# Hybrid pool, GLA and attention block: softmax division moved from the probabilities to the outputs, once a pair and half, through a DRAM round trip on GpSimd's queue

## The chip, the cores and the metric

The kernel runs on one core of a Trainium2 chip. Its time is the device time of one launch, in microseconds (us), and lower is better. Engines are named as in the profile: PE is TensorE's matrix unit and PEld its weight loads, DVE is VectorE, ACT is ScalarE, POOL is GpSimd, and SP is the queue that issues most of the transfers. "L615" is line 615 of the kernel before.

## What is computed

One transformer-like layer on 1024 tokens of width 1024, all in fp32: RMSNorm, one input projection, three token mixers side by side (pooling, gated linear attention, forgetting attention), an output projection, a residual, then RMSNorm, a SwiGLU feed-forward of width 2816, a residual and a last RMSNorm. The change touches the forgetting attention alone: eight heads of 64, causal, with a softmax.

```
def fox_mixer(q, k, v, f_logit, b_f):            # 8 heads of 64, 1024 tokens
    logf = log_sigmoid(f_logit + b_f); F = cumsum(logf over time)
    s = (q * 64**-0.5) @ k.T + F[query] - F[key]
    s = where(key <= query, s, -inf)
    p = softmax(s)                               # exp(s - max) / sum
    return p @ v
...
mix = concatenate([y_pool, y_gla, y_fox]); x = x + mix @ w_o
```

## The kernel before

fp32 products are made of three matmuls on a high and a low part of each operand (hi·hi, hi·lo, lo·hi), so nearly every operand is split once by ACT (copy to fp32r) and once by DVE or POOL (the rest). The program is written in one order, and a scheduler with a timeline of its own then sets the order on each engine; rings and pools of buffers limit it. What follows goes by that final order.

The attention works on pairs of heads, p = 0 to 3; a is the head of the pair (its rows are 64a to 64a+63). For one pair `fox_attend` makes eight items (a, m), one for every 256 queries. An item does this, in `fox_item`:

- scores: for its two blocks of 128 queries, PE multiplies Q with K and with KL, K's low part (tile `s`, L575, L576), and adds the causal mask (L578); DVE adds the key's F, stores into `pb` and takes the minimum (L580); ACT makes exp, and sums each row (L584).
- division: DVE's reciprocal of the two sums (L587), then `pb` times it, the first block on POOL (L590), the second on DVE (L592).
- turning: PE transposes `pb` in pieces of 128x128 (tile `pt`, L601), ACT and DVE split them into `pp` (L603, L604).
- output: PE multiplies with V's high and low parts side by side into the one bank of tag `o` (L615); ACT copies its lower half out (L618, `ot`), and DVE adds the upper half (L621, `y`). With that the bank is free for the next item.

PSUM holds 3 banks for `s`, 2 for `pt`, 1 for `o` and 2 for `gm` (projections). In SBUF the rings are "p" (six `pb`), "pp" (three), "fb" (two, the rows of F), "wr" (two raw weights on their way in) and "w" (their split parts).

Around the attention of pair p stand projections that PE can do in between: `zq`, `zk` of the next pair (48 matmuls of 512 columns each), `psv` (the values of heads 4 to 7, 192 matmuls of 256 columns, with the weights `wfv_0`, `wfv_1`, made between pairs 1 and 2 in the program), and `pxa`, `pxb`, the output projection (192 matmuls of 512 columns each). Their raw weights come through the ring "wr"; POOL makes the low part of zq, zk and wfv (L119). A finished pair's output `y` is split by ACT (L273) and DVE (L274) and stored in DRAM (`keep_mix`); the last pair's output is split at once into `last_mix` (L624, L625). After the output projection each block of 128 tokens is normed (`norm2`: L720, L722 with the gain row `ln2b` that POOL's queue loads at L714) and turned by PE (`n2pt`, L727). Then come the feed-forward's matmuls (`m`, L774, and `d`, L1030).

Of the kernel before, what the change touches and what calls it, by code (L numbers as in the profile page):

```python
# [18 lines left out]
P = 128  # L19
# [12 lines left out]
def tile_hybrid_block(ctx: ExitStack, tc, x, w_fv, w_gv, w_zt, w_o, w_gu, w_down, ln, w_pool, w_a3, chans, b_f, consts, out):  # L32
    nc = tc.nc
    ACT, DVE, POOL, PE, SP = nc.scalar, nc.vector, nc.gpsimd, nc.tensor, nc.sync
# [4 lines left out]
    dpool = ctx.enter_context(tc.tile_pool(name="dp", bufs=1, space=bass.MemoryType.DRAM))  # L39
# [10 lines left out]
    def G(name, dtype=F32):  # L50
        i = idle.pop(0)
        t_ = big.tile([P, 1024], dtype, tag=f"g{i}", name=name)
        where[name] = i
        return t_

    def free(*names):
        for n in names:
            idle.append(where.pop(n))

    def R(name, dtype=F32, tag="p"):  # L60

# [50 lines left out]
    def PS(tag, name):  # L112
        return pst.tile([P, 512], F32, tag=tag, name=name, bufs=BANKS[tag])
# [22 lines left out]
    def half(name, dtype=F32):  # L136
        return rng.tile([P, 512], dtype, tag="tmp", name=name, bufs=2)
# [25 lines left out]
    def names_T(name):  # L163
        return [f"{name}{k}_{c}_{h}" for k in range(4) for c in range(2) for h in range(2)]
# [105 lines left out]
    def keep_mix(k, y):  # L270

        hi = G(f"mh{k}", F32R)
        ACT.activation(hi, y, AF.Copy)  # L273
        DVE.tensor_tensor(out=y, in0=y, in1=f(hi), op=ALU.subtract)  # L274
# [17 lines left out]
    last_mix = []  # L292
# [253 lines left out]
                    POOL.tensor_copy(t_[a][own[1 - a], csl], f(t_[a][own[a], csl]))  # L546
        return Q, K, KL

    def fox_item(p, a, m, ops, fb, V, Y):

        Q, K, KL = (t_[a] for t_ in ops)
        nm = f"{p}_{a}_{m}"
        rows = slice(64 * a, 64 * a + 64)
        Pb, Ws = [], []
        l, rl = S(f"l{nm}", 2), S(f"rl{nm}", 2)
        for i in range(2):
            qb = 2 * m + i
            W = P * (qb + 1)
            nh = 1 if W <= 512 else 2
            w = W // nh  # L560
            qs = slice(qb * P, (qb + 1) * P)
            mn = S(f"mn{nm}_{i}")
            if m >= 2:
                pb = R(f"pb{nm}_{i}")
            elif i == 0:
                pb2 = R(f"pb{nm}")
                pb = pb2[:, 0:512]
            else:
                pb = pb2[:, 512:1024]
            top = 3.0e38  # L570
            for h in range(nh):
                s = PS("s", f"s{nm}_{i}_{h}")
                ks = slice(h * w, (h + 1) * w)
                last = h == nh - 1
                PE.matmul(s[:, 0:w], Q[:, qs], K[:, ks], start=True, stop=False)  # L575
                PE.matmul(s[:, 0:w], Q[:, qs], KL[:, ks], start=False, stop=not last)  # L576
                if last:
                    PE.matmul(s[:, w - P:w], identr, maskr, start=False, stop=True)  # L578
                t_ = mn if last else S(f"mw{nm}_{i}")
                DVE.tensor_tensor_reduce(out=pb[:, ks], in0=s[:, 0:w], in1=fb[:, ks], scale=1.0, scalar=top,  # L580
                                         op0=ALU.add, op1=ALU.min, accum_out=t_)
                top = t_[:, 0:1]

            ACT.activation(pb[:, 0:W], pb[:, 0:W], AF.Exp, bias=mn[:, 0:1], scale=-1.0, accum_out=l[:, i:i + 1])  # L584
            Pb.append(pb)
            Ws.append(W)
        DVE.reciprocal(rl, l)  # L587
        for i, (pb, W) in enumerate(zip(Pb, Ws)):
            if i == 0:
                POOL.tensor_tensor(out=pb[:, 0:W], in0=pb[:, 0:W], in1=rl[:, 0:1].broadcast_to([P, W]), op=ALU.mult)  # L590
            else:
                DVE.tensor_scalar(out=pb[:, 0:W], in0=pb[:, 0:W], scalar1=rl[:, 1:2], scalar2=None, op0=ALU.mult)  # L592
        o = PS("o", f"o{nm}")
        for n in range(m + 1):
            pt = PS("pt", f"pt{nm}_{n}")
            pp = R(f"pp{nm}_{n}", F32R, tag="pp")
            cut = P if n == m else 0
            for b in range(2):
                for i in range(b if cut else 0, 2):
                    o0 = 256 * b + P * i - cut * b  # L600
                    PE.transpose(pt[:, o0:o0 + P], Pb[i][:, (2 * n + b) * P:(2 * n + b + 1) * P], ident)  # L601
            w = 512 - cut
            ACT.activation(pp[:, 0:w], pt[:, 0:w], AF.Copy)  # L603
            DVE.tensor_tensor(out=pp[:, 512:512 + w], in0=pt[:, 0:w], in1=f(pp[:, 0:w]), op=ALU.subtract)  # L604
            for b in range(2):
                kb = 2 * n + b
                o0 = cut * b
                v_ = V[p % 2][kb // 4][:, kb % 4, a]
                ph = pp[:, 256 * b:512 - o0] if b else pp[:, 0:256]
                pl = pp[:, 768:1024 - o0] if b else pp[:, 512:768]  # L610
                both = (o[:, o0:256], v_.rearrange("p s e -> p (s e)"), ph)
                high = (o[0:64, o0:256], v_[:, 0], pl)
                last = kb == 2 * m + 1
                for n_, args in enumerate((high, both) if last else (both, high)):
                    PE.matmul(*args, start=(kb == 0 and n_ == 0), stop=(last and n_ == 1))  # L615
        tmp = half(f"ot{nm}")
        ot, oy = tmp[0:64, 0:256], tmp[:, 256:512]
        ACT.activation(ot, o[64:128, 0:256], AF.Copy)  # L618
        if p < 3:
            oy = Y[:, m * 256:(m + 1) * 256]  # L620
        DVE.tensor_tensor(out=oy[rows], in0=o[0:64, 0:256], in1=ot, op=ALU.add)  # L621
        if p == 3:
            hi, lo = (last_mix[m // 2][rows, h, (m % 2) * 256:(m % 2 + 1) * 256] for h in range(2))
            ACT.activation(hi, oy[rows], AF.Copy)  # L624
            POOL.tensor_tensor(out=lo, in0=oy[rows], in1=f(hi), op=ALU.subtract)  # L625

    def fox_attend(p, ops, V, Y):
        fbs = []
        for a in range(2):
            fb = R(f"fb{p}_{a}", tag="fb")  # L630
            SP.dma_start(fb, Fd[2 * p + a:2 * p + a + 1, :].broadcast_to([P, T]))
            fbs.append(fb)
        for a, m in ([(a, m) for a in range(2) for m in range(4)] if p < 3 else [(a, m) for m in (1, 0, 3, 2) for a in range(2)]):
# [40 lines left out]
    V = fox_values(0, (B.within(1), o_[0][:1], o_[0][1:], o_[1][:1], o_[1][1:] + B.turned(0), B.turned(1), (), ()))  # L674
    for k in range(8):
        keep_wo(k)
    ops = fox_qk(0)
    free("gv0", "gv1", "attb0", "attb1")
    for p in range(4):
        if p == 3:  # L680
            last_mix += [G(f"mix7_{g}", F32R).rearrange("p (h t) -> p h t", h=2) for g in range(2)]
        Y = G(f"y{p}") if p < 3 else None
        fox_attend(p, ops, V, Y)
        done = [f"{n}{p}_{a}" for n in ("q", "k", "kl") for a in range(2)] + [f"v{p}_{i}" for i in range(2)]
        if p == 1:
# [12 lines left out]
    ws = [fetch_wo(k) for k in range(4)]
# [284 lines left out]
    sums = {}  # L983
# [139 lines left out]
```

## Time and profile before

| what | before |
|---|---|
| median of 3 runs | 1176.26 us (1174.48 to 1177.74) |
| the profiled execution | 1175.42 us |
| its span, first to last instruction | 1173.7 us |
| granted TensorE clock, mean | 0.992 |
| busy: PE, DVE, ACT, POOL | 1136.0, 828.2, 536.0, 340.4 us |
| first projections and gated mixer | 0 to 202 us |
| attention with its projections and the output projection | 202 to 541 us |
| feed-forward | 541 to 1173 us |

Busy times are sums over the span, and the stages have different limits, so a share of busy time says little by itself: an instruction that leaves an engine is worth time only where PE was waiting for that engine. A row of a view reads: line, engine, operation, output<-input, shape, count | busy us, mean ns | idle time of that engine just ahead, and what ended it.

### The profile page before, as it was taken

Reading aid. Unit: us, or ns where it says so; the run is one execution under the profiler, and the core shown is the slowest. Engines: PE = TensorE matmul, PEld = TensorE weight load, DVE = VectorE, ACT = ScalarE, POOL = GpSimd, SP = SyncE. Lnnn points to the kernel's source line nnn. Section 1 sums busy time; section 2 is a strip of 40 time slices with the busy share of each in tenths; the row PEclk is TensorE's granted clock in tenths of the full one; section 3 lists DMA queues with packets and bytes.
Section 4 is the critical chain, followed back from the end, with each engine's and each line's share of the span. In section 5 each row is a group of like instructions: output and inputs, shape, how many; then the busy total and the mean of one; then the engine's idle time right before and its main releaser. Section 6 shows DMA issues by size and latency. Waiting matters only on the chain.

```text
span 1173.7 us, 15953 instructions
## 1 busy us (share of the span) xinstructions
PE 1136.0 (97%) x5928; PEld 958.5 (82%) x5928; DVE 828.2 (71%) x1365; ACT 536.0 (46%) x970; POOL 340.4 (29%) x260
## 2 busy tenths in 40 slices
PE   6999998999999999998999999999999999999996
PEld 5877878889978888886888888888888888888875
DVE  6697364387746866579997767767686685876686
ACT  6454233466654644456453433444344344334345
POOL 2231123343322413210302221022201370660784
PEclk9999999999999999999999999999999999999999
DMA  7121184411203734431323332242314688333233
GB/s 250 37 73 52 59 295 174 176 39 35 91 18 126 305 132 159 173 112 46 117 86 129 101 115 88 101 134 82 135 54 152 224 322 293 103 95 102 86 112 143
DMA packets 57692, 150.45 MB, mean 128 GB/s; under 512 B 5080, under 2 KB 5512, under 8 KB 57616
## 3 DMA queue, kind: packets, MB, share of 16 engines
q1 hardware_dynamic: 57184, 147.87, 36.5%
q0 software_dynamic: 432, 1.57, 0.4%
q8 instruction: 46, 0.75, 0.3%
q14 instruction: 30, 0.25, 0.1%
HBM read 105.09 MB, written 44.34 MB: 127 GB/s over the span
## 4 chain that ended last, share of the span: by engine, by line
PE 76%; DVE 4%; DMA 1%; issue 1%; POOL 1%; ACT 1%; SPq 0%; POOLq 0%; DVEq 0%; ACTq 0%
PE m L774 36%; PE d L1030 15%; PE pxa L144 4%; PE pxb L144 3%; PE o L615 3%; PE pt L601 2%; PE psv L152 2%; PE s L575 1%; PE s L576 1%; PE zq3p L152 1%; PE zq0p L152 1%; PE zq2p L152 1%; PE zk1p L152 1%; PE zk2p L152 1%; PE zk0p L152 1%
## 5 line engine op out<-in xcount | busy, mean ns | idle before, releaser
L774 PE MATMUL m<-hA_0h,wr 128*128 128x512 f32 x616 | 214.7, 391 | 1.2 <-ACT hr L729 1.2
L774 PE MATMUL m<-hA_1h,wr 128*128 128x512 f32 x616 | 214.9, 389 | 0.0
L774 PEld LDWEIGHTS m<-hA_0h,wr 128*128 128x128 f32 x616 | 116.1, 189 | 25.8 <-ACT hr L729 1.6
L774 PEld LDWEIGHTS m<-hA_1h,wr 128*128 128x128 f32 x616 | 115.8, 188 | 24.2
L1030 PE MATMUL d<-lw,ha 128*128 128x512 f32 x308 | 119.9, 389 | 0.9 <-DVE lw L880 0.9
L774 PE MATMUL m<-hA_0l,wr 128*128 128x512 f32 x308 | 120.3, 391 | 0.0
L774 PE MATMUL m<-hA_1l,wr 128*128 128x512 f32 x308 | 119.9, 389 | 0.0
L1030 PE MATMUL d<-hw,ha 128*128 128x512 f32 x308 | 119.3, 389 | 0.0
L1030 PE MATMUL d<-hw,la 128*128 128x512 f32 x308 | 118.4, 389 | 0.0
L756 ACT ACTIVATE wr<-ws 128x512 fp32r<-128x512 f32 x110 | 69.5, 632 | 101.5 <-DVE ws L755 50.1
L826 POOL TENSOR_TENSOR cg<-cu,cu 128x512 f32<-128x512 f32 x11 | 19.7, 1795 | 302.8 <-DVE cu L803 266.7
L757 DVE TENSOR_TENSOR wr<-ws,wr 128x512 fp32r<-128x512 f32 x110 | 76.8, 704 | 20.6 <-ACT wr L756 20.5
L880 DVE TENSOR_TENSOR la<-ra,ha 128x1024 fp32r<-128x1024 f32 (+1 forms) x42 | 57.2, 1368 | 32.0 <-ACT ha L879 24.7
L590 POOL TENSOR_TENSOR pb<-pb,rl 128x128 f32<-128x128 f32 (+3 forms) x32 | 39.0, 1222 | 117.5 <-DVE rl L587 108.9
L872 POOL TENSOR_TENSOR rw<-wd,wd 128x512 f32<-128x512 f32 x33 | 59.0, 1815 | 47.7 <-PE d L1030 47.6
L879 ACT ACTIVATE ha<-ra 128x1024 fp32r<-128x1024 f32 (+1 forms) x42 | 41.3, 987 | 65.6 <-DMA ra<-cd 56.8
L1030 PEld LDWEIGHTS d<-lw,ha 128*128 128x128 f32 x308 | 57.8, 188 | 13.3 <-DVE lw L880 1.3
L604 DVE TENSOR_TENSOR pp<-pt,pp 128x512 fp32r<-128x512 f32 (+1 forms) x80 | 50.2, 631 | 25.7 <-ACT pp L603 25.3
L774 PEld LDWEIGHTS m<-hA_0l,wr 128*128 128x128 f32 x308 | 58.1, 189 | 12.0
L774 PEld LDWEIGHTS m<-hA_1l,wr 128*128 128x128 f32 x308 | 58.0, 188 | 12.0
L1030 PEld LDWEIGHTS d<-hw,la 128*128 128x128 f32 x308 | 57.8, 188 | 12.1
L1030 PEld LDWEIGHTS d<-hw,ha 128*128 128x128 f32 x308 | 57.8, 188 | 11.9
(398 smaller groups left out, 2690.6 us busy)
## 6 DMA issues: line engine op xcount, KB each, us to landing
ra<-cd SPq DMA_DIRECT2D x35, 512.0 KB, 3.9
wu<-in_w_gu_dram SPq DMA_DIRECT2D x22, 512.0 KB, 4.6
wg<-in_w_gu_dram SPq DMA_DIRECT2D x22, 512.0 KB, 3.7
wd<-in_w_down_dram SPq DMA_DIRECT2D x22, 512.0 KB, 6.4
mix<-mixs SPq DMA_DIRECT2D x14, 512.0 KB, 5.3
cd<-cg SPq DMA_DIRECT2D x11, 512.0 KB, 6.3
cd<-cs SPq DMA_DIRECT2D x11, 512.0 KB, 3.4
cd<-cu SPq DMA_DIRECT2D x11, 512.0 KB, 3.3
```

Source lines behind the costliest of these rows:

```text
L144: PE.matmul(ps, a, b, start=(n == 0), stop=(n == last))
L152: PE.matmul(ps, a, b, start=(i == 0 and n == 0), stop=(i == len(terms) - 1 and n == 2))
L590: POOL.tensor_tensor(out=pb[:, 0:W], in0=pb[:, 0:W], in1=rl[:, 0:1].broadcast_to([P, W]), op=ALU.mult)
L604: DVE.tensor_tensor(out=pp[:, 512:512 + w], in0=pt[:, 0:w], in1=f(pp[:, 0:w]), op=ALU.subtract)
L615: PE.matmul(*args, start=(kb == 0 and n_ == 0), stop=(last and n_ == 1))
L756: ACT.activation(hi, src, AF.Copy)
L757: DVE.tensor_tensor(out=lo, in0=src, in1=f(hi), op=ALU.subtract)
L774: PE.matmul(ps, a, b, start=(n == 0), stop=(n == 11))
L872: POOL.tensor_tensor(out=raw_[:, j * 512:j * 512 + 512], in0=wd[h0, j0 + j][:, e0, :], in1=wd[h1, j0 + j][:, e1, :], op=op)
L879: ACT.activation(hi[:, sl], src, AF.Copy)
L880: DVE.tensor_tensor(out=lo[:, sl], in0=src, in1=f(hi[:, sl]), op=ALU.subtract)
L1030: PE.matmul(banks[t], a[:, o], b[:, ns], start=(j0 + j == 0 and m == 0), stop=(j0 + j == NF // 2 - 1 and m == 2))
```

## The change

`pb` is no longer divided. The sums of a pair are kept in one tile of 16 columns, and the outputs are divided at the end of the pair, in two halves g of 512 tokens: `divide` takes the reciprocal of the eight columns (DVE), turns them with PE (128x8 to 8x128, through a `pt` bank), copies them out with ACT, writes the 4 KB to DRAM on POOL's queue, reads them back twice with a step of zero over 64 partitions (tile `rb`, in a buffer of the ring "wr"), and multiplies `y` by them on POOL. The last pair makes its first half after its first four items; its split into `last_mix` comes after the division and is made once a half. The copy of the lower half of the `o` bank goes from ACT to DVE. In the program, `divide` of pair p stands behind the projections of pair p+1 and ahead of `keep_mix`.

```
-    def fox_item(p, a, m, ops, fb, V, Y):
+    def fox_item(p, a, m, ops, fb, V, Y, sums):
...
-            ACT.activation(pb[:, 0:W], pb[:, 0:W], AF.Exp, bias=mn[:, 0:1], scale=-1.0, accum_out=l[:, i:i + 1])
+            ACT.activation(pb[:, 0:W], pb[:, 0:W], AF.Exp, bias=mn[:, 0:1], scale=-1.0, accum_out=sums[:, col(a, qb)])
...
-        DVE.reciprocal(rl, l)
-        for i, (pb, W) in enumerate(zip(Pb, Ws)):
-            if i == 0:
-                POOL.tensor_tensor(out=pb[:, 0:W], in0=pb[:, 0:W], in1=rl[:, 0:1].broadcast_to([P, W]), op=ALU.mult)
-            else:
-                DVE.tensor_scalar(out=pb[:, 0:W], in0=pb[:, 0:W], scalar1=rl[:, 1:2], scalar2=None, op0=ALU.mult)
...
-        ACT.activation(ot, o[64:128, 0:256], AF.Copy)
-        if p < 3:
-            oy = Y[:, m * 256:(m + 1) * 256]
-        DVE.tensor_tensor(out=oy[rows], in0=o[0:64, 0:256], in1=ot, op=ALU.add)
+        ot = half(f"ot{nm}")[0:64, 0:256]
+        DVE.tensor_copy(ot, o[64:128, 0:256])
+        DVE.tensor_tensor(out=Y[rows, m * 256:(m + 1) * 256], in0=o[0:64, 0:256], in1=ot, op=ALU.add)
+    Ld = dpool.tile([4, 2, 2, 512], F32, name="Ld")
+    def divide(p, Y, sums, g):
+        rw = R(f"rb{nm}", tag="wr")
+        rl, rt, rb, gs = S(f"rl{nm}", 8), rw[0:8, 512:640], rw[:, 0:512], slice(g * 512, g * 512 + 512)
+        DVE.reciprocal(rl, sums[:, 8 * g:8 * g + 8])
+        pt = PS("pt", f"ptl{nm}")
+        PE.transpose(pt[0:8, 0:P], rl, ident)
+        ACT.activation(rt, pt[0:8, 0:P], AF.Copy)
+        POOL.dma_start(Ld[p, g].rearrange("a (q t) -> (a q) t", t=P), rt)
+        for a in range(2):
+            POOL.dma_start(rb[64 * a:64 * a + 64, :], Ld[p, g, a:a + 1, :].broadcast_to([64, 512]))
+        POOL.tensor_tensor(out=Y[:, gs], in0=Y[:, gs], in1=rb, op=ALU.mult)
         if p == 3:
-            hi, lo = (last_mix[m // 2][rows, h, (m % 2) * 256:(m % 2 + 1) * 256] for h in range(2))
-            ACT.activation(hi, oy[rows], AF.Copy)
-            POOL.tensor_tensor(out=lo, in0=oy[rows], in1=f(hi), op=ALU.subtract)
+            ACT.activation(last_mix[g][:, 0], Y[:, gs], AF.Copy)
+            POOL.tensor_tensor(out=last_mix[g][:, 1], in0=Y[:, gs], in1=f(last_mix[g][:, 0]), op=ALU.subtract)
...
+            if p == 3 and (a, m) == (1, 0):
+                divide(p, Y, sums, 0)
+        if p == 3:
+            divide(p, Y, sums, 1)
...
         if p < 3:
             free(*done)
+            for g in range(2):
+                divide(p, Y, sums, g)
             keep_mix(4 + p, Y)
```

The scheduler puts the engines' instructions into another order than before. In the rows below, lines of the changed kernel carry its own numbers (L574, L575, L577 are the scores, L593 the transposes, L607 the output, L583 exp, L595 the split of `pt`, L624 to L634 are `divide`); the lines up to L548 and inside `keep_mix` (L273, L274) are the same in both. A number behind a tile's name only tells its instances apart.

PE, second half of pair 0, before: the projection `psv` stands between the attention's matmuls while pair 0 (`o_0_3`, `s_1_2`: head and block) is still being worked on.

```order
L601 MATMUL pt_0_3_1_2266<-ident,pb_0_3_1_2238 128x128
L576 MATMUL s_1_2_1_0_2403<-kl_1_1928,q_1_1924 128x384
L575 MATMUL s_1_2_1_1_2408<-k_1_1926,q_1_1924 128x384
L576 MATMUL s_1_2_1_1_2408<-kl_1_1928,q_1_1924 128x384
L578 MATMUL s_1_2_1_1_2408<-maskr,identr 128x128
L152 MATMUL psv_0_3174<-wfv_1h,hT_0_0_93 128x256
L152 MATMUL psv_0_3174<-wfv_1l,hT_0_0_93 128x256
L152 MATMUL psv_0_3174<-wfv_1h,hT_0_1_94 128x256
```

PE, the same projection in the changed kernel: its first matmul stands in the attention of pair 1, with 84 matmuls between it and `ptl_1` of pair 0's `divide`.

```order
L593 MATMUL pt_0_3_2_2861<-ident,pb_0_3_0_2811 128x128
L593 MATMUL pt_0_3_2_2861<-ident,pb_0_3_1_2824 128x128
L152 MATMUL psv_0_3117<-wfv_0h,hT_0_0_85 128x256
L152 MATMUL psv_1_3146<-wfv_0h,hT_0_0_85 128x256
L607 MATMUL o_0_3_2836<-pp_0_3_1_2850,v_0_1511 128x256
L607 MATMUL o_0_3_2836<-pp_0_3_1_2850,v_0_1511 64x256
```

What moved: from the last `zk1p` matmul to that first `psv` the changed order holds 247 attention matmuls, the two transposes of `divide`, and no projection; in the same 249 places before, 107 were projection matmuls.

POOL at that place, before: `wfv_0l` is made between two divisions of pair 0.

```order
L590 TENSOR_TENSOR pb_0_0_2073<-pb_0_0_2073,rl_0_0_2071 128x128
L590 TENSOR_TENSOR pb_0_1_2108<-pb_0_1_2108,rl_0_1_2106 128x384
L119 TENSOR_TENSOR wfv_0l<-wfv_0r,wfv_0h 128x1024
L590 TENSOR_TENSOR pb_0_2_0_2155<-pb_0_2_0_2155,rl_0_2_2153 128x640
L546 CAST k_0_2540<-k_0_2540 64x512
```

POOL there in the changed kernel:

```order
L628 DMA Ld<-rb_0_2642 8x128
L628 DMA Ld<-rb_1_2652 8x128
L630 DMA rb_0_2642<-Ld 64x512 x2
L630 DMA rb_1_2652<-Ld 64x512 x2
L631 TENSOR_TENSOR y_2066<-y_2066,rb_0_2642 128x512
L631 TENSOR_TENSOR y_2066<-y_2066,rb_1_2652 128x512
L119 TENSOR_TENSOR wfv_0l<-wfv_0r,wfv_0h 128x1024
L119 TENSOR_TENSOR wfv_1l<-wfv_1r,wfv_1h 128x1024
```

What moved: `wfv_0l` and `wfv_1l` stand behind the whole division of pair 0, and since the two `rb` take both buffers of the ring "wr", SP's loads of `wfv_0r` and `wfv_1r` also wait for the two multiplications.

ACT, during pair 3, in the changed kernel: `mh` is the split of pair 2's divided `y` (L273), and behind it stands the work of pair 3's items.

```order
L627 ACTIVATE rb_0_4092<-ptl_0_4095 8x128
L627 ACTIVATE rb_1_4102<-ptl_1_4105 8x128
L583 ACTIVATE pb_0_3_1_4295,l_4124<-pb_0_3_1_4295,mn_0_3_1_4294 128x1024
L595 ACTIVATE pp_0_1_0_4142<-pt_0_1_0_4141 128x512
L595 ACTIVATE pp_0_1_1_4154<-pt_0_1_1_4153 128x384
L583 ACTIVATE pb_1_3_0_4359,l_4124<-pb_1_3_0_4359,mn_1_3_0_4358 128x896
L595 ACTIVATE pp_1_1_0_4184<-pt_1_1_0_4183 128x512
L595 ACTIVATE pp_1_1_1_4196<-pt_1_1_1_4195 128x384
L595 ACTIVATE pp_0_0_0_4226<-pt_0_0_0_4225 128x384
L273 ACTIVATE mh_4112<-y_3516 128x1024
L583 ACTIVATE pb_1_3_1_4372,l_4124<-pb_1_3_1_4372,mn_1_3_1_4371 128x1024
L595 ACTIVATE pp_1_0_0_4256<-pt_1_0_0_4255 128x384
```

ACT there before:

```order
L603 ACTIVATE pp_0_1_0_4201<-pt_0_1_0_4200 128x512
L618 ACTIVATE ot_1_3_4023<-o_1_3_3975 64x256
L603 ACTIVATE pp_0_1_1_4213<-pt_0_1_1_4212 128x384
L584 ACTIVATE pb_0_3_1_4367,l_0_3_4351<-pb_0_3_1_4367,mn_0_3_1_4366 128x1024
L273 ACTIVATE mh_4168<-y_3553 128x1024
L584 ACTIVATE pb_1_3_0_4438,l_1_3_4435<-pb_1_3_0_4438,mn_1_3_0_4437 128x896
```

What moved: before, L273 waited for the last item's add on DVE; now it waits for POOL's two multiplications, seven instructions behind the copies that start the round trip. The same stands in pair 0, where twelve instructions lie between.

POOL at the end of the attention, before: `ln2b`, the gain row for the second norm, is loaded while the last items are still divided.

```order
L625 TENSOR_TENSOR mix_0_4173<-ot_1_0_4346,mix_0_4173 64x256
L714 DMA ln2b<-in_ln_dram 128x1024
L590 TENSOR_TENSOR pb_1_2_0_4594<-pb_1_2_0_4594,rl_1_2_4592 128x640
L625 TENSOR_TENSOR mix_1_4174<-ot_0_3_4430,mix_1_4174 64x256
L625 TENSOR_TENSOR mix_1_4174<-ot_1_3_4514,mix_1_4174 64x256
L102 TENSOR_TENSOR n_v<-n2ss_4997,epst 128x1
```

POOL there in the changed kernel:

```order
L628 DMA Ld<-rb_1_4565 8x128
L630 DMA rb_1_4565<-Ld 64x512 x2
L631 TENSOR_TENSOR y_4119<-y_4119,rb_1_4565 128x512
L634 TENSOR_TENSOR mix_1_4118<-y_4119,mix_1_4118 128x512
L731 DMA ln2b<-in_ln_dram 128x1024
L102 TENSOR_TENSOR n_v<-n2ss_4911,epst 128x1
```

What moved: `ln2b` stands behind the whole last division, which starts when the last item is done; on PE, 24 `pxa` and 48 `pxb` matmuls stand between that item and the first `n2pt`.

More of the change, by code (lines that the diff above doesn't have):

```diff
@@ L553, in fox_item @@
         rows = slice(64 * a, 64 * a + 64)
-        Pb, Ws = [], []
-        l, rl = S(f"l{nm}", 2), S(f"rl{nm}", 2)
+        Pb = []
         for i in range(2):
@@ L582, in fox_item @@
                 top = t_[:, 0:1]
-            ACT.activation(pb[:, 0:W], pb[:, 0:W], AF.Exp, bias=mn[:, 0:1], scale=-1.0, accum_out=l[:, i:i + 1])
+            ACT.activation(pb[:, 0:W], pb[:, 0:W], AF.Exp, bias=mn[:, 0:1], scale=-1.0, accum_out=sums[:, col(a, qb)])
             Pb.append(pb)
-            Ws.append(W)
-        DVE.reciprocal(rl, l)
-        for i, (pb, W) in enumerate(zip(Pb, Ws)):
-            if i == 0:
-                POOL.tensor_tensor(out=pb[:, 0:W], in0=pb[:, 0:W], in1=rl[:, 0:1].broadcast_to([P, W]), op=ALU.mult)
-            else:
-                DVE.tensor_scalar(out=pb[:, 0:W], in0=pb[:, 0:W], scalar1=rl[:, 1:2], scalar2=None, op0=ALU.mult)
         o = PS("o", f"o{nm}")
@@ L615, in fox_item, with col @@
                     PE.matmul(*args, start=(kb == 0 and n_ == 0), stop=(last and n_ == 1))
-        tmp = half(f"ot{nm}")
-        ot, oy = tmp[0:64, 0:256], tmp[:, 256:512]
-        ACT.activation(ot, o[64:128, 0:256], AF.Copy)
-        if p < 3:
-            oy = Y[:, m * 256:(m + 1) * 256]
-        DVE.tensor_tensor(out=oy[rows], in0=o[0:64, 0:256], in1=ot, op=ALU.add)
+        ot = half(f"ot{nm}")[0:64, 0:256]
+        DVE.tensor_copy(ot, o[64:128, 0:256])
+        DVE.tensor_tensor(out=Y[rows, m * 256:(m + 1) * 256], in0=o[0:64, 0:256], in1=ot, op=ALU.add)
+    Ld = dpool.tile([4, 2, 2, 512], F32, name="Ld")
+    def col(a, qb):
+        c = 8 * (qb // 4) + 4 * a + qb % 4
+        return slice(c, c + 1)
+    def divide(p, Y, sums, g):
+        nm = f"{p}_{g}"
+        rw = R(f"rb{nm}", tag="wr")
[8 more added lines that the diff above has]
+        POOL.tensor_tensor(out=Y[:, gs], in0=Y[:, gs], in1=rb, op=ALU.mult)
         if p == 3:
-            hi, lo = (last_mix[m // 2][rows, h, (m % 2) * 256:(m % 2 + 1) * 256] for h in range(2))
-            ACT.activation(hi, oy[rows], AF.Copy)
-            POOL.tensor_tensor(out=lo, in0=oy[rows], in1=f(hi), op=ALU.subtract)
+            ACT.activation(last_mix[g][:, 0], Y[:, gs], AF.Copy)
+            POOL.tensor_tensor(out=last_mix[g][:, 1], in0=Y[:, gs], in1=f(last_mix[g][:, 0]), op=ALU.subtract)
     def fox_attend(p, ops, V, Y):
@@ L632, in fox_attend @@
             fbs.append(fb)
+        sums = S(f"l{p}", 16)
         for a, m in ([(a, m) for a in range(2) for m in range(4)] if p < 3 else [(a, m) for m in (1, 0, 3, 2) for a in range(2)]):
-            fox_item(p, a, m, ops, fbs[a], V, Y)
+            fox_item(p, a, m, ops, fbs[a], V, Y, sums)
+            if p == 3 and (a, m) == (1, 0):
+                divide(p, Y, sums, 0)
+        if p == 3:
+            divide(p, Y, sums, 1)
+        return sums
     x3d = [dpool.tile([P, D], F32, name=f"x3d{tb}") for tb in range(NT)]
@@ L681, in tile_hybrid_block @@
             last_mix += [G(f"mix7_{g}", F32R).rearrange("p (h t) -> p h t", h=2) for g in range(2)]
-        Y = G(f"y{p}") if p < 3 else None
-        fox_attend(p, ops, V, Y)
+        Y = G(f"y{p}")
+        sums = fox_attend(p, ops, V, Y)
         done = [f"{n}{p}_{a}" for n in ("q", "k", "kl") for a in range(2)] + [f"v{p}_{i}" for i in range(2)]
@@ L693, in tile_hybrid_block @@
             free(*done)
+            for g in range(2):
+                divide(p, Y, sums, g)
             keep_mix(4 + p, Y)
-            free(f"y{p}")
+        free(f"y{p}")
     ws = [fetch_wo(k) for k in range(4)]
```

## The prediction

> **What bounds the kernel now.** I read the busy shares first, then who PE waited for, then single stretches of the attention.
>
> ```profile
> span 1173.7 us, 15953 instructions
> PE 1136.0 (97%) x5928; PEld 958.5 (82%) x5928; DVE 828.2 (71%) x1365; ACT 536.0 (46%) x970; POOL 340.4 (29%) x260
> ...
> PE n1s L180 <- DVE n1sq L174: 10.4, 1, 10.4
> PE zq0p L152 <- DVE v L529: 3.5, 1, 3.5
> PE zq3p L152 <- DVE kl L544: 2.5, 1, 2.5
> PE o L615 <- DVE pp L604: 0.7, 2, 0.3
> ...
> 255.00:263.00 8.00, 8.00 (x61) 7.51 (x60) 7.41 (x15) 5.53 (x13) 5.07 (x4) 1.00 0.07 26
> 385.00:397.00 12.00, 11.57 (x76) 9.80 (x75) 10.92 (x30) 8.07 (x19) 5.14 (x8) 1.00 1.04 404
> ```
>
> PE is the bound. Its waits (us in all, times, longest) are few, and the attention's own are the zq3p row, at the end of pair 1, and 0.7 us. The two stretches (length; busy PE, PEld, DVE, ACT, POOL; clock) show why: at 255 to 263 projections stand between the attention's matmuls and PE never rests. At 385 to 397, where attention stands almost alone, DVE is 91% busy (10.92 of 12) and PE begins to miss. So work taken from DVE, ACT or POOL is worth something only where PE lacks projections to fill with.
>
> **What is removed.**
>
> ```profile
> L590 POOL TENSOR_TENSOR pb<-pb,rl 128x128 f32<-128x128 f32 (+3 forms) x32 | 39.0, 1222 | 117.5 <-DVE rl L587 108.9 <-PE pt L601 8.3
> L592 DVE TENSOR_SCALAR pb<-pb,rl 128x256 f32<-128x256 f32 (+3 forms) x32 | 29.3, 915 | 0.9
> L618 ACT ACTIVATE ot<-o 64x256 f32<-64x256 f32 x32 | 12.2, 382 | 22.6 <-PE o L615 22.2
> ```
>
> 39.0 us leave POOL and 29.3 leave DVE; 12.2 leave ACT and come back on DVE as 32 copies. Under PE's filler all of it is worth nothing. The gain lies where PE starved:
>
> ```profile
> 346.42 0.39 PE L615 MATMUL o<-pp,v 128*128 128x256 f32 x1
> ...
> 353.19 0.79 PE L152 MATMUL zq3p<-hT,zq3h 128*128 128x512 f32 x2 [2.55 <-DVE kl L544]
> ...
> 357.41 0.39 PE L152 MATMUL zq3p<-hT,zq3l 128*128 128x512 f32 x1
> ...
> 349.00:352.00 3.00, 1.30 (x8) 1.00 0.00 0
> 352.00:355.00 3.00, 1.81 (x5) 0.79 0.17 67
> 355.00:358.00 3.00, 3.00 (x10) 0.64 0.70 283
> ...
> 379.13 0.89 PE o L615 x8
> 504.71 5.49 PE pxb L144 x24
> ```
>
> From 346.42 to 353.19 PE does the last 16 output matmuls of pair 1 (0.111 us each by the 379.13 row) and 7 transposes, 2.5 us of work in 6.8: 4.2 lost. Then the granted clock is 0.79 and 0.64, and 11 zq3p matmuls take 4.2 us where 512 columns cost 0.229 (504.71 row): 1.7 more. In the new order `psv` stands in that tail, so it is covered; the new order must still have K's copies before pair 2. I count **-5** of these 6, and **-1** for the PE that missed at 391 to 397.
>
> The Trainium skill (TensorE: Matmul & The Clock Gate, Part 1) says the array falls to half rate after an idle window of about 3.4 us and returns after as long a busy one. The trace agrees: the rows of 0.79 and 0.64 follow 349 to 353.
>
> **The dense stretch.** 247 attention matmuls now run with no projection (before, 107 of 249 were projections). A pair has 72 transposes, 80 output and 64 score matmuls, 216 in all, so this is 1.14 pairs.
>
> ```profile
> 392.45 0.40 DVE L621 TENSOR_TENSOR y<-o,ot 64x256 f32<-64x256 f32 x1
> 392.78 0.67 DVE L604 TENSOR_TENSOR pp<-pt,pp 128x512 fp32r<-128x512 f32 x1
> 393.38 0.60 DVE L580 CUSTOM_DVE_ANT_0 pb<-s,fb,mw 128x384 f32<-128x384 f32 x1
> ...
> L604 DVE TENSOR_TENSOR pp<-pt,pp 128x512 fp32r<-128x512 f32 (+1 forms) x80 | 50.2, 631 | 25.7 <-ACT pp L603 25.3
> L580 DVE CUSTOM_DVE_ANT_0 pb<-s,fb 128x128 f32<-128x128 f32 (+3 forms) x64 | 33.5, 534 | 8.5 <-issue 4.7 <-PE pt L601 2.1 <-PE s L578 0.7
> L580 DVE CUSTOM_DVE_ANT_0 pb<-s,fb,mw 128x320 f32<-128x320 f32 (+3 forms) x32 | 20.6, 645 | 2.9 <-PE s L578 2.2
> L584 ACT ACTIVATE pb<-pb,mn 128x128 f32<-128x128 f32 (+3 forms) x64 | 49.5, 774 | 37.7 <-DVE mn L580 36.5 <-DVE rl L587 1.0
> L603 ACT ACTIVATE pp<-pt 128x512 fp32r<-128x512 f32 (+1 forms) x80 | 43.5, 554 | 42.1 <-PE pt L601 33.8 <-PE o L615 6.3 <-PE s L578 0.5
> ```
>
> DVE's rows follow each other 0.07 us sooner than they last (392.45, 392.78, 393.38). A pair costs DVE 20 x 0.56 (L604), 24 x 0.49 (L580), and 16 x 0.33 for copy and add: 11.2 + 11.8 + 5.3 = 28.3 us. The copy isn't in the trace; it lies between ACT's 0.38 and the add's 0.33, and I take the add, the same tile on the same engine. PE: 72 x 0.11, 80 x 0.11 and 20480 score columns at 0.229/512: 7.9 + 8.9 + 9.1 = 25.9. For 1.14 pairs that is 32.3 and 29.5; at DVE's 91% it takes 35.5, so PE loses **+6**. Ends: +3 (DVE never idle) and +9 (85%).
>
> **The round trip.** It is new: every `y` now waits for it, and things queue behind it.
>
> ```profile
> 466.13 0.65 POOL L714 DMA_DIRECT2D ln2b<-in_ln_dram  x1 [6.45 <-PE pxa L144]
> ...
> DMA to landing us min/median/max: 6.8/6.8/6.8
> ...
> DMA to landing us min/median/max: 3.8/3.8/3.8
> ...
> cd<-cu SPq DMA_DIRECT2D x11, 256.0 KB, 2.1
> ln1b<-in_ln_dram POOLq DMA_DIRECT2D x1, 512.0 KB, 8.2
> wfv_0r<-in_w_fv_dram SPq DMA_DIRECT2D x2, 512.0 KB, 4.2
> ...
> L826 POOL TENSOR_TENSOR cg<-cu,cu 128x512 f32<-128x512 f32 x11 | 19.7, 1795 | 302.8 <-DVE cu L803 266.7 <-issue 36.1
> L273 ACT ACTIVATE mh<-y x3: 1043/1052/1057, 299.3 to 435.3; 128x1024 fp32r<-128x1024 f32 x3
> L274 DVE TENSOR_TENSOR y<-y,mh x3: 1207/1221/1226, 301.0 to 436.9; 128x1024 f32<-128x1024 f32 x3
> L722 DVE SCALAR_TENSOR_TENSOR n2sq<-xa,n_r,ln2b 128x1024 f32<-128x1024 f32 x8 | 10.2, 1279 | 4.5 <-POOL n_r L103 4.4
> 240.54 2.41 POOL L119 TENSOR_TENSOR wfv_0l<-wfv_0r,wfv_0h 128x1024 fp32r<-128x1024 f32 x1 [2.04 <-ACT wfv_0h L118]
> ```
>
> The two landing lines are those of `ln2b` and of the like row `lnfb`. For a pair's two halves, counted from `ptl_1`: 0.25 for ACT's copy (an estimate, under L618's 0.38 for its 8x128); POOL issues Ld at 0.65 each, the first lands after 2.1 (the smallest store, 256 KB); four `rb` issues, 0.65 each; the second lands after 3.8 (the shortest of the three broadcasts on POOL's queue, for a quarter of their size); two multiplications of 1.8. That is 3.0, 4.3, 8.1, then 9.9 and 11.7 us; with `rb` landing in 2.1 or 8.2, 10.0 or 16.1. What stands behind it:
>
> Pair 0: ACT has six exps and six splits ahead of L273, by L584 and L603 some 8.2 us, and so idles; DVE has about 11.5 of the dense stretch ahead of L274. L273 ends at 12.8 and L274 at 14.0, so the `o` bank, whose add stands behind L274, is free near 14.3 instead of 11.5. The load of `wfv_0r` starts at 9.9 and lands at 14.1; ACT's split and POOL's 2.41 follow near 18; before, that row was done at 243, long ahead. Together **+4** (0 to 8).
>
> Pair 2, done during pair 3: seven ACT instructions, 5.2 us, stand ahead of L273, so ACT idles 6.5. PE has 83 matmuls up to the next half's `ptl_0`, of which 24 are `pxa` (5.5 us), 12.8 us; behind these it needs transposes whose buffer ACT frees only after L273 (12.8), an exp of 1.3, a split and DVE, near 15.8: **+3** (0 to 7). The same queue's wait for the last pair's first half: ACT's work fills nearly all of it, **+0.5** (0 to 2).
>
> Pair 1 has 96 matmuls of 512 columns (22 us) behind it on PE; only POOL's copies of K queue behind the multiplications and zq3l: **+1** (0 to 3).
>
> The end: one half takes 0.25 + 2.1 + 1.3 + 3.8 + 1.8 = 9.3, ACT's and POOL's split 0.6 and 1.8, so `ln2b` is issued at 11.7, lands 6.8 later, and L722 ends at 19.8. PE reaches the first `n2pt` after 0.5 and 72 x 0.229, at 17.0: **+2.5** (0 to 8).
>
> Eight small transposes at 0.11: **+1**. What else SP and POOL carry (the loads of `xa`, `mix`, F) keeps at least one buffer's lead; nothing there is counted.
>
> **Sum.** -5 - 1 + 6 + 4 + 3 + 0.5 + 1 + 2.5 + 1 = +12. The profiled execution took 1175.4 (span 1173.7 and 1.7 around it), 0.9 under the median of the runs, 1176.26. 1175.4 + 12 = **1187.4 us**.
>
> The Trainium skill (DMA: Bandwidth & Descriptors, Anatomy of one DMA — SWDGE) puts a transfer of this queue at about 2.0 us plus bytes/436e3, so 2.3 for an `rb` and 3.2 for 512 KB. The trace's 3.8, 6.8 and 8.2 lie above it. By the rule the chain is 10.2 and `ln2b` lands 3.6 us sooner, and as an estimate from that page the sum would be near 1181.
>
> **Rivals.**
> Relief wins: if DVE's 28.3 us a pair are met without idling and the round trip hides, PE starves nowhere, and with the gain of 6, the small transposes and 3 in the dense stretch it is 1175.4 - 6 + 1 + 1 = 1171 to 1173. For it: DVE at 91% already bounds 385 to 397. Against it: 32.3 exceeds 29.5 even then. It decides if the trip stays under about 8 us.
> No change: the trip costs 3 us in all and the dense stretch 3, which eats the 6: 1176. The point is a landing near 2.5 us.
> Long trip: `rb` lands like `ln1b`, 8.2. Then pair 0, pair 2 and the end each wait 4.4 us longer, over 3 us at a time, and each pays the 1.7 of the slow clock: 12 + 3 x 6.1 = +30, 1205.
> The bank isn't emptied faster: in half of the items another DVE instruction stands between copy and add, 0.6 us or more of `o` each; in the dense stretch that is some 5 items, +3 to the forecast, 1190.
>
> **Chances.** Forecast and the held bank (1179 to 1196) 0.55; long trip 0.15; no change 0.15; relief 0.15. About 0.3% is what a measurement here can tell from no change, 3.5 us. Faster is the relief, 0.15; the same 0.15; slower 0.70. The range takes in the relief's upper end and part of the long trip: 1172 to 1199; the likeliest case's own is 1179 to 1196.
>
> **What would show it.** PE's busy share in a window of 20 us in pair 0's end falls below 0.95, with waits for DVE `pp` or `y`; L273 on ACT waits for POOL's L631 for 2 to 7 us in pairs 0 and 2; the first `psv` waits for `wfv`; `n2pt` or L722 waits for `ln2b`; the tail at 346 to 358 is gone. The forecast is wrong if `rb` lands in about 2 us, or if PE stays full in the dense stretch.

## The result, and the profile after

The changed kernel takes 1219.24 us (median of 4 runs, 1217.84 to 1220.29), the kernel before 1176.35 (4 runs beside it): a ratio of 1.0358, interval 1.0343 to 1.0372. The forecast was 1187.4, at most 1199. It is slower, as forecast, but by 43 us and not by 12.

The page of the changed kernel, and PE's longest waits in it (us in all, times, longest):

```profile
span 1218.5 us, 15902 instructions
PE 1146.4 (94%) x5936; PEld 962.9 (79%) x5936; DVE 814.4 (67%) x1341; ACT 521.5 (43%) x940; POOL 322.4 (26%) x254
...
PE pxa L144 <- DVE xa L673: 17.8, 2, 16.2
PE n2pt L744 <- DVE n2sq L739: 5.8, 1, 5.8
PE pt L593 <- DVE pp L596: 5.4, 8, 1.0
...
PE o L607 <- DVE y L610: 2.9, 3, 2.1
PE pxb L144 <- DMA wo6h<-wod: 2.5, 1, 2.5
```

DVE, ACT and POOL have become idler, and so has PE: it waits. The first row was in no step of the forecast. `xa` is a block of the input that a `pxa` result is added to; nothing of the change touches it.

Three stretches hold the loss, and one a gain. First before, then after (length; busy PE, PEld, DVE, ACT, POOL; clock):

```profile
260.00:310.00 50.00, 49.94 (x403) 48.81 (x402) 40.50 (x112) 33.55 (x80) 15.70 (x14) 1.00 0.16 54
340.00:362.00 22.00, 18.76 (x97) 15.46 (x96) 9.26 (x20) 8.67 (x18) 8.03 (x9) 0.92 0.19 72
440.00:470.00 30.00, 30.00 (x173) 26.13 (x171) 20.42 (x50) 13.41 (x28) 8.83 (x8) 1.00 0.50 165
480.00:530.00 50.00, 50.00 (x259) 42.09 (x258) 33.76 (x44) 28.30 (x60) 9.72 (x16) 1.00 0.32 116
```

```profile
260.00:310.00 50.00, 42.13 (x284) 37.15 (x283) 39.51 (x107) 32.11 (x70) 13.06 (x14) 0.93 0.30 95
340.00:362.00 22.00, 20.68 (x92) 16.85 (x91) 5.94 (x9) 7.50 (x13) 15.02 (x15) 1.00 0.36 120
440.00:470.00 30.00, 25.25 (x143) 20.63 (x142) 19.77 (x50) 13.45 (x27) 8.55 (x12) 1.00 0.69 236
480.00:530.00 50.00, 27.91 (x123) 21.57 (x122) 13.21 (x22) 6.46 (x12) 5.48 (x8) 0.80 0.36 121
...
500.00:510.00 10.00, 4.92 (x12) 3.90 (x13) 1.29 (x2) 0.00 (x0) 0.00 (x0) 0.50 0.26 83
```

Length less busy PE times clock is what PE lost, as an estimate: 10.8 us in the first pair's end (260 to 310), 4.8 during the last pair (440 to 470), 27.7 at the end of the attention (480 to 530), all near 0 before; at the end of pair 1 (340 to 362) 1.3 instead of 4.7. With 2.3 more at the last `n2pt` (5.8 against 3.5 before) that is 42 of the 45 us by which the span grew. The last row is why the stall cost more than its length: the clock is at 0.50 behind it.

The end of the attention, in the chain of waits of the changed kernel (start, us, what):

```profile
487.16 0.99 PE o L607 x8
488.29 0.28 ACT rb L627
...
488.85 1.57 DMA Ld<-rb
...
490.70 0.55 POOL rb L630
491.25 4.99 DMA rb<-Ld
496.37 1.26 POOL y L631
...
498.37 1.27 POOL mix L634
499.66 4.59 DMA xa<-in_x_dram
504.34 0.70 DVE xa L673
505.08 7.71 PE pxa L144 x22
512.80 8.47 DMA wo6l<-wod
```

The last division runs from 488 to 499.6, about as long as forecast (from `ptl` to the divided `y` 9.6 us, forecast 9.3). But PE has the 24 `pxa` matmuls of the last block to do, which need nothing of it, and stands still. What ties them to it is the line of `xa`: it is issued at 499.66, when L634 has read `y3` for the last time. General buffers go round first in, first out: a name takes the one that was given back longest ago. Before, the last pair had no `y3`; now it takes buffer 5 and gives it back in the program just ahead of the output projection, where the 23rd name asked for, `xa6`, gets it. Until its load lands, `pxa` of block 6 cannot leave its bank, `gm` has two banks, and PE's queue stands behind. Then the next: five of the six halves of `wo5` to `wo7` are handed buffers that the last `pxa` still reads, before as after, and now no attention is left to cover their loads.

What the forecast had put at this end, a wait of `n2pt` for `ln2b` behind the last division, isn't there. Two rows of the changed kernel, and PE's longest wait of that kind in a kernel that divides nothing (e8, below):

```profile
511.45 0.59 POOL L731 DMA_DIRECT2D ln2b<-in_ln_dram  x1 [11.82 <-PE pxa L144]
...
584.61 1.94 PE L744 MATMUL n2pt<-ident,n2sq 128*128 128x128 f32 x8 [5.75 <-DVE n2sq L739]
...
PE n2pt L721 <- DVE n2sq L716: 5.8, 1, 5.8
```

POOL issues `ln2b` when a `pxa` ends, not when the division does, and the first `n2pt` starts at 530.94 without a wait. The 5.8 us belong to the last block of tokens, 85 us behind the division. Without any division (e8) that wait is 5.8 too, and with all of it (e2) 3.5: it is not the division's, and what sets it stays open.

At the first pair's end, one row or two of each engine (the second number is the length; in brackets the wait and who ended it):

```profile
297.89 1.06 ACT L273 ACTIVATE mh<-y 128x1024 fp32r<-128x1024 f32 x1 [1.16 <-POOL y L631]
...
298.98 1.22 DVE L274 TENSOR_TENSOR y<-y,mh 128x1024 f32<-128x1024 f32 x1 [0.78 <-ACT mh L273]
300.23 0.42 DVE L610 TENSOR_TENSOR y<-o,ot 64x256 f32<-64x256 f32 x1
...
300.79 0.36 PE L607 MATMUL o<-pp,v 128*128 128x256 f32 x1 [2.13 <-DVE y L610]
...
295.93 0.33 SPq L117 DMA_DIRECT2D wfv_0r<-in_w_fv_dram  x1
...
302.06 0.48 PE L152 MATMUL psv<-wfv_0h,hT 128*128 128x256 f32 x2
```

This went as forecast: L273 waits for the division, L274 for L273, the add that frees the `o` bank stands behind L274, and PE waits 2.13 for it. SP loads `wfv_0r` at 295.93, when the first multiplication has ended, so `psv` starts at 302, behind the 249 places of the order that hold no projection. Only the size differs: L273 waits 1.2 us, where 2 to 7 were expected, and in pair 2 it doesn't wait for the division at all.

### The profile page after: what moved, and what is told of

Its sections match the earlier page's. It is cut to its first block, busy times and chain, and to the rows that moved or that the text cites. A ratio compares the mean times of both kernels' runs of the same rounds, so it can differ in the third digit from the quotient of the medians.

```text
span 1218.5 us, 15902 instructions
## 1 busy us (share of the span) xinstructions
PE 1146.4 (94%) x5936; PEld 962.9 (79%) x5936; DVE 814.4 (67%) x1341; ACT 521.5 (43%) x940; POOL 322.4 (26%) x254
## 4 chain that ended last, share of the span: by engine, by line
PE 67%; DVE 5%; DMA 4%; POOL 4%; issue 3%; ACT 1%; POOLq 0%; DVEq 0%; ACTq 0%
PE m L791 34%; PE d L1047 12%; PE pxa L144 4%; PE psv L152 2%; PE o L607 2%; PE pt L593 2%; PE pxb L144 2%; POOL rw L889 2%; PE zq0p L152 1%; PE zk1p L152 1%; PE zk3p L152 1%; PE s L574 1%; PE zk0p L152 1%; PE zq3p L152 1%; PE zq1p L152 1%
## 5 line engine op out<-in xcount | busy, mean ns | idle before, releaser
L595 ACT ACTIVATE pp<-pt 128x512 fp32r<-128x512 f32 (+1 forms) x80 | 42.6, 551 | 53.7 <-PE pt L593 41.7
L897 DVE TENSOR_TENSOR lw<-rw,hw 128x1024 fp32r<-128x1024 f32 (+1 forms) x30 | 48.8, 1638 | 20.4 <-ACT hw L896 20.3
```

Source lines behind the costliest of these rows:

```text
L897: DVE.tensor_tensor(out=lo[:, sl], in0=src, in1=f(hi[:, sl]), op=ALU.subtract)
```

## The experiments

| run | us | ratio to the kernel before | interval |
|---|---|---|---|
| the changed kernel | 1219.24 | 1.0358 | 1.0343 to 1.0372 |
| e1: y3 given back after pxa | 1209.41 | 1.0298 | 1.0269 to 1.0326 |
| e2: rb of pairs 0 to 2 not in wr | 1215.33 | 1.0339 | 1.0322 to 1.0356 |
| e3: both | 1210.04 | 1.0294 | 1.0279 to 1.0309 |
| e4: copy on ACT | 1217.75 | 1.0364 | 1.0348 to 1.0381 |
| e5: y3 given back at the end | 1196.84 | 1.0177 | 1.0162 to 1.0193 |
| e6: e5, rb not in wr, wr handed on last | 1191.07 | 1.0130 | 1.0114 to 1.0146 |
| e7: e5, division spread on the chip | 1186.30 | 1.0094 | 1.0078 to 1.0109 |
| e8: before, without division | 1175.10 | 0.9993 | 0.9984 to 1.0002 |
| e9: last pair as before | 1184.22 | 1.0079 | 1.0063 to 1.0095 |
| e10: before, copy on DVE | 1183.04 | 1.0066 | 1.0052 to 1.0079 |
| e11: on the chip, last pair as before, copy on ACT | 1179.88 | 1.0043 | 1.0030 to 1.0055 |
| e12: before, pair 1's second head reversed | 1172.01 | 0.9980 | 0.9968 to 0.9992 |
| e13: e8 with copy on DVE | 1176.26 | 1.0006 | 0.9997 to 1.0015 |
| e14: trip in pairs 0 to 2, last pair as before, copy on ACT | 1190.55 | 1.0123 | 1.0109 to 1.0137 |
| e15: e14, rb of pair 2 in wr | 1175.83 | 1.0001 | 0.9990 to 1.0012 |

Each ratio is to runs of the kernel before taken beside it, whose medians lie between 1174.4 and 1176.4. Across rows the ratios are the safer measure: by them the gains of 22, 28 and 35 us below are some 21, 27 and 33.

**Whose buffer.** The theory was that loads are late because they are handed buffers of the division; the rival, that the trip itself is what PE waits for.

```
         if p < 3: ... keep_mix(4 + p, Y)
-        free(f"y{p}")
+            free(f"y{p}")
...                                     # after the loop over the pxa:
+    free("y3")
```

> The changed kernel, with the buffer of y3 given back after the last pxa instead of ahead of them, so that xa6 gets a buffer that has long been free. Theory (buffers): the load of xa6 stood behind the last division only because it was handed y3's buffer; pxa 6 and 7 then fill PE during that division. The wait of 16.2 us for xa goes, and most of the slow clock behind it: 1190 to 1203 us. Rival (the trip): PE needs the last division's result there in any case; the wait turns up at pxb, and the time stays at 1212 or more.

It gained 10 us, between the two. The trace says why: PE's waits, the queue of SP, and POOL's last row.

```profile
PE pxb L144 <- DMA wo7h<-wod: 14.6, 1, 14.6
...
509.33 0.52 SPq L662 DMA_DIRECT2D mix<-mixs  x1
511.33 0.32 SPq L289 DMA_DIRECT2D wo7h<-wod  x1
...
510.04 1.26 POOL L634 TENSOR_TENSOR mix<-y,mix 128x512 fp32r<-128x512 f32 x1 [0.74 <-ACT mix L633]
```

The wait had only changed its name. Given back later, buffer 5 goes to `wo7h`, whose load starts 0.03 us after the end of L634.

```
-        rw = R(f"rb{nm}", tag="wr")
+        rw = G(f"rb{nm}") if p < 3 else R(f"rb{nm}", tag="wr")
...
+        if p < 3: free(f"rb{nm}")
```

> The changed kernel, with rb of pairs 0 to 2 in general buffers instead of the ring wr. Theory (buffers): the loads of wfv no longer wait for the division, psv comes back into pair 0, and of the 15.7 us that PE lost at 260 to 310 some 12 go; the stall at the end of pair 1 (7 us before) comes back in part: 1205 to 1213 us. Rival (the trip): the wait of ACT and DVE for the divided y, or DVE's own load, is what starved PE there: 1215 or more.

> Both edits on buffers together; the round trip through DRAM stays whole, all 8 times. Theory (buffers): the two gains add, 1178 to 1192 us, within 1.5% of the kernel before. Rival (the trip): 1200 or more.

e2 gained 4 us, which is the rival's edge. Its trace doesn't speak for the rival, though:

```profile
260.00:310.00 50.00, 49.28 (x386) 47.36 (x385) 38.07 (x109) 30.64 (x72) 10.57 (x13) 1.00 0.19 64
440.00:470.00 30.00, 23.52 (x133) 19.69 (x132) 17.91 (x43) 12.32 (x24) 7.63 (x9) 0.94 0.83 265
...
PE pxa L144 <- DMA mix<-mixs: 5.9, 3, 2.9
```

`psv` comes back into pair 0, and what PE loses from 260 to 310 falls from 10.8 us (the 15.7 expected with does not come out of the rows) to 0.7, with the trip as it was. But as much is lost elsewhere: 4.4 instead of 1.3 at the end of pair 1, where the stall is back, 4.2 instead of none at 380 to 400, and 7.9 instead of 4.8 at 440 to 470. There the edit made a new tie: the two `rb` of pair 2, now general buffers, are handed to `mix2` and `mix3` of the second half, and PE waits 5.4 us for these loads. e3 is by its number the rival's too; in it `wo7h` still got `y3`'s buffer, and PE waited 13.0 us for it.

> In the run with y3's buffer given back after the pxa, the wait did not go, it moved: 14.6 us for wo7h, which was handed y3's buffer instead. Here it is given back only when all pxb are done, so no load waits for y3. Theory (buffers): 13 us of those go: 1192 to 1200 us. Rival (the trip): the wait moves once more, to the last division itself or to ln2b: 1205 or more.

```
-    free(*[f"wo{k}{h}" ...], "ln2b", ...)          # after the last pxb
+    free(*[f"wo{k}{h}" ...], "ln2b", "y3", ...)
```

Now it goes: 22.4 us under the changed kernel, from the place of one line that gives a buffer back. The trip, the multiplications and the copy are all as they were. The same stretch, and PE's longest wait in it:

```profile
480.00:530.00 50.00, 44.71 (x233) 37.70 (x232) 24.04 (x36) 14.10 (x32) 7.67 (x14) 0.97 0.43 153
...
PE pxb L144 <- DMA wo5h<-wod: 4.9, 1, 4.9
```

PE loses 6.6 us there instead of 27.7, and the wait that is left is for a load whose buffer the last `pxa` read.

> As the run before, with rb of pairs 0 to 2 in general buffers, and the ring wr handed on last, so that neither a load of wfv nor one of mix is handed a buffer of rb. The round trip stays whole. Theory (buffers): 1186 to 1196 us, what is left being the trip's own cost on ACT and DVE in pair 2 and the stall at the end of pair 1. Rival: the buffers' parts do not add, 1200 or more.

5.8 us more. With both, 28 of the 43 us are gone, and the round trip is still made eight times. One tie was left against the expectation: as in e2, `mix2` and `mix3` of the second half are handed the `rb` of pair 2, and PE waits 4.8 us for the second of them.

**The last pair.**

```
+        if p == 3: # reciprocal, POOL and DVE divide pb, as before; no Y3, no divide(3, ...)
```

> The changed kernel, with the last pair's pb divided as before (reciprocal, POOL and VectorE) and no y3; pairs 0 to 2 keep the trip, with rb in the ring wr. Theory: of the 43 us the last pair's part is what PE lost at 480 to 530, 28 us, and a few of what it lost at 440 to 470: 1184 to 1192 us. Rival (every trip costs alike): a quarter of 43 goes, 1208.

35 of the 43 us, the good end of its range. Dividing the last pair at its end was most of the change's price; three quarters of the trips, with `rb` in `wr`, cost the rest together with the copy. PE is busy 49.00 of the 50 us from 480 to 530, and all 30 from 440 to 470: part of what the forecast put down to pair 2's trip was the last pair's own.

**The trip.**

```
-  transpose rl; ACT copies 8x128; POOL: store, two broadcast loads; POOL multiplies y by rb
+  ACT spreads rl to 128x512; four transposes of 128x128 into a pt bank; DVE multiplies y by the bank
```

> No trip through DRAM: the reciprocals are spread by ACT to 128x512 (two copies), turned by four transposes of 128x128 into a bank of pt, and VectorE multiplies y from there; y3's buffer given back at the end. A half then takes some 2.5 us instead of 9 to 12. If the trip's length is what is left beside the buffers: 1176 to 1186 us. If DVE's load or the order is: within 4 us of the run with neither buffer, 1188 or more.

4.8 us under e6, just above the range. It still divides the last pair at its end, and its `rx` lies in the small ring of `ot`, not in general buffers: what went may again be a buffer's part.

> Pairs 0 to 2 divided on the chip once a pair (reciprocals spread by ACT, turned by four transposes, multiplied by VectorE from the bank), the last pair as before, the copy on ACT: no DRAM, no y3, no rb in the ring wr. Theory (buffers and the trip made all of the 43 us; the division on pb was covered): 1174 to 1180 us, the same as before. If moving the division off pb were worth anything: 1172 or less. If y's wait costs even without a trip: 1182 or more.

1179.9: inside the range, but by the interval slower than the kernel before, by 5 us. The 24 transposes are 2.6 of it (0.11 each), and PE is busy 17.97 of the 22 us from 340 to 362, against 18.76 before; the cause of the rest stays open. No gain from taking the division off `pb` shows.

> The trip through DRAM for pairs 0 to 2, rb in general buffers, the last pair as before, the copy on ACT: the same as the run with the division on the chip, but for the way the reciprocals take. That one was at 1179.9. If the trip's length costs in the first three pairs: 1184 or more. If it hides there once no buffer hangs on it: 1176 to 1182.

1190.6, as if the trip cost 10.7 by itself. But its trace shows again a load tied to the division: POOL's multiplication in pair 2, SP's load of `mix`, PE.

```profile
441.21 1.27 POOL L648 TENSOR_TENSOR y<-y,rb 128x512 f32<-128x512 f32 x1 [5.68 <-DMA rb<-Ld]
...
442.51 0.52 SPq L677 DMA_DIRECT2D mix<-mixs  x1
...
447.31 0.50 PE L144 MATMUL pxa<-wo3h,mix 128*128 128x512 f32 x1 [2.34 <-DMA mix<-mixs]
```

The multiplication ends at 442.48, the load starts at 442.51: `rb` of pair 2, now a general buffer, had been handed to `mix3` of the second half, and the other one to `xa4`. The run did not part what it was made to part; e2, e3 and e6 share that edit.

```
-        rw = G(f"rb{nm}") if p < 3 else R(f"rb{nm}", tag="wr")
+        rw = G(f"rb{nm}") if p < 2 else R(f"rb{nm}", tag="wr")
```

> The run of the trip in pairs 0 to 2 still had a buffer hanging on it: the rb of pair 2 had been handed on to a load of mix and one of xa, and SP stood still from 434 to 452. Here rb of pair 2 stays in the ring wr, which nothing else uses by then; rb of pairs 0 and 1 in general buffers, the last pair as before, the copy on ACT. The trip and the run with the division on the chip (1179.9) then differ only by the trip. If those buffers were what cost 10 us: 1178 to 1184. If the trip's length costs by itself: 1187 or more.

1175.83 against 1175.85: below its range, the same as the kernel before. Six trips through DRAM, all the multiplications, the division off `pb` in three pairs of four: nothing gained, nothing lost. And yet the trip is no shorter; the rows of `rb` in e15 (who waited; landing, the store's and the loads' together):

```profile
  POOL rb L647: 4.9, 2
  ACT mh L273: 4.7, 2
...
DMA to landing us min/median/max: 1.6/3.1/8.5
```

L273 waits 4.7 us for it, where the changed kernel had 1.2, and it doesn't show in the time.

**The copy, and what the division was worth.**

```
-        DVE.tensor_copy(ot, o[64:128, 0:256])
+        ACT.activation(ot, o[64:128, 0:256], AF.Copy)
```

> The changed kernel, with the copy of the o bank's lower half back on ACT. If DVE's load (32 copies of 0.43 us, 14 us) is what starves PE in the attention, 3 to 7 us come back: 1212 to 1216 us. If buffers and the trip are the cause, it is within 2 us of 1219. If the copy on DVE empties the bank sooner, it is slower than 1219 by 2 us or more.

1217.75 against 1219.24, and the ratios' intervals overlap: in the changed kernel the copy costs nothing that shows.

> The kernel before with one edit, the copy of the o bank's lower half on VectorE instead of ACT. By the theory that neither the bank nor VectorE's 14 us bound anything under the projections: within 0.3% of the kernel before, 1173 to 1179 us. If the copy costs VectorE what PE lacks: 1180 or more. If it frees the bank sooner to any use: 1172 or less.

But alone in the kernel before it costs 8.6 us. In its trace, DVE, POOL and PE at 307:

```profile
307.83 2.26 DVE L592 TENSOR_SCALAR pb<-pb,rl 128x256 f32<-128x256 f32 x1
310.01 0.28 DVE L529 TENSOR_TENSOR v<-psv,v 128x128 fp32r<-128x128 f32 x1
...
306.99 2.95 POOL L119 TENSOR_TENSOR zq2l<-zq2r,zq2h 128x1024 fp32r<-128x1024 f32 x1 [2.56 <-ACT zq2h L118]
...
310.34 0.73 PE L152 MATMUL zq2p<-hT,zq2h 128*128 128x512 f32 x2 [1.97 <-DVE v L529]
```

In this order the division of a `pb` (L592) meets POOL's L119 and takes 2.26 us, where the same shape takes 0.33 at the least before; behind it stands the split that frees a `gm` bank, and PE waits 1.97. The clock is at 0.61 in the 4 us from 312. By the estimate above PE loses 3.8 us at 300 to 320, where before it lost almost none, and 6.3 at 340 to 370 instead of 4.5; together that is most of the 6.1 us by which this execution's span is longer.

> The kernel before without its division (the output is left undivided): the most that taking the division off pb can bring. If the 6 us that PE lost at the end of pair 1 and at 391 to 397 come from the division's load on DVE and POOL: 1168 to 1172 us. If they come from the order (K's copies behind the attention): within 0.3% of the kernel before, 1173 to 1179.

> The kernel before without its division (the output is left undivided) and with the copy on VectorE. The copy alone cost 8 us, and in its trace PE stood still at 308 to 310 behind a division on VectorE (L592) that took 2.26 us instead of 0.33 while POOL worked. If that meeting of copy, division and POOL is the cost: without divisions the copy is free, 1172 to 1178 us. If the copy's own 14 us on VectorE are: 1181 or more.

Without any division (the output is left undivided) the kernel takes what it took, 1175.1 (0.9993), and then the copy is free too (1.0006). So there was nothing to be had by moving the division, and the copy's price needs a division beside it; that L592 against POOL is the whole of the 8.6 us is not shown, and the losses above put it at some 3.8.

**The stall at the end of pair 1.** `kl2` is handed the two buffers of pair 1's values, which the pair's last output matmuls read.

```
-  [(a, m) for a in range(2) for m in range(4)]
+  [(0, m) for m in range(4)] + [(1, m) for m in (3, 2, 1, 0)]       # pair 1 only
```

> The kernel before, with pair 1's second head taken from its longest item to its shortest, so that the last item of the pair, after which KL of pair 2 gets the buffers of pair 1's values, is short. Theory (the stall at 346 to 358 is a wait for these two buffers): the stall of 7 us shrinks by 2 to 5, 1171 to 1175 us. Rival (it is the last item's own chain of exp, division and splits): no change, 1175 to 1179.

1172.01, ratio 0.9980 (0.9968 to 0.9992): a little faster than both kernels. The splits that make `kl2`, before and here:

```profile
L544 DVE TENSOR_TENSOR kl<-zk2p,k x4: 672/684/694, 350.7 to 353.1; 64x512 fp32r<-64x512 f32 x4
...
L544 DVE TENSOR_TENSOR kl<-zk2p,k x4: 672/684/695, 346.6 to 352.2; 64x512 fp32r<-64x512 f32 x4
```

They start 4 us sooner, and PE's wait of 2.5 for them is gone.

## Why the prediction was wrong

By its own steps, with what PE lost by the rows above:

- **Buffers, the step that failed.** "What else SP and POOL carry (the loads of `xa`, `mix`, F) keeps at least one buffer's lead; nothing there is counted." It looked at where the loads stand in SP's queue, and not at whose buffer each one is handed. A new name in a first-in, first-out pool shifts every later one by a place, and the one that was given back last went to a load that PE needed. It measured 22.4 us (e5), and with the rest of the last pair's division 35 (e9).
- **The end, +2.5 (0 to 8).** Only the trip's length was right, 9.6 us for 9.3, and that with luck in its parts: the landing of `rb` took 4.99 for 3.8, the store 1.57 for 2.1, the multiplication 1.26 for 1.8. The cover given to it failed, 24 `pxa` and 48 `pxb` running on: they could not run, and PE lost 27.7 us, of which e5 leaves 6.6. The wait that was forecast, of `n2pt` for `ln2b`, did not come: `ln2b` hung on a `pxa`, as its row before already showed. (19.8 less 17.0 is also 2.8, not 2.5.)
- **Dense stretch and pair 0, +6 and +4.** 10.8 us lost, by the ways that were named: DVE near its limit, L274 before the bank's add, `wfv` behind the multiplications. Size and way were near, and e2 tells which of them carried the others: with `rb` out of the ring "wr", and so `psv` in its old place, 0.7 is left.
- **Pair 2 and the last pair's first half, +3 and +0.5.** 4.8 lost, but e9 shows it to be the last pair's doing rather than pair 2's: with the last pair as before nothing is lost at 440 to 470, and in the changed kernel L273 of pair 2 never waited for the multiplications. That 4.8 lies near the 3.5 is luck.
- **Pair 1, -5, -1, +1.** At 340 to 362 PE lost 1.3 by the row above, against 4.7 by the same view before: 3.4 gained. That `psv` covers the stall was right. The division itself has no part in it (e8 keeps it, e12 shortens it): `psv` covers it because `psv` is late, and the dense stretch paid for that.
- **The chance for relief, 0.15,** rested on these 6 us too. No run that only took division away gained.
- **The rivals.** "Long trip" came nearest in time (1205) with the wrong cause: `rb` landed in 4.99 in the last pair and in 3.0 in the median, not 8.2. Nothing in my list had a late transfer that has nothing to do with the change.
- **The range** ended at 1199, since every case in it priced the trip and none the general buffers.

The estimate from the Trainium skill (DMA: Bandwidth & Descriptors, Anatomy of one DMA — SWDGE) of 2.3 us for an `rb` stands against 2.9 to 6.4 here, 3.0 in the median.

## What to carry to other kernels

When a change keeps a buffer longer or asks for one more, list before and after which name gets which buffer, and who reads it last; a load that has nothing to do with the change may be the one that waits. A fix that only moves the wait to another name (e1) is a sign of this, and a run meant to be free of it should be read for it too (e14). A long trip off the critical path was free here once nothing that PE needed was handed its buffers or stood behind it without filler (e15), and taking work off engines that PE did not wait for was worth nothing (e8). A wait that lies where the forecast put one must still be looked up in time: the 5.8 us at `n2pt` came 85 us after the division.

## What was not expected of the hardware

The division L592 on DVE takes 0.33 us at the least for 128x256, and 2.26 when POOL's L119 runs beside it (e10); it ends within 0.2 us of POOL's row. It is not the only place: in the kernel before the eight of this shape take 0.33 to 1.58 us, the longest beside two of POOL's L590. The Trainium skill (SBUF — State Buffer, Who interferes with whom) has a rule for it: one kind of DVE instruction and POOL share a pair of ports, and the one that comes second waits for the whole of the other. The trace agrees in these places; no run here measured it alone.
